# FFN weights of four chunks: split into two parts once and kept in DRAM, instead of split anew for every tile

## The chip, the cores and the metric

The kernel runs on one core of a Trainium2 chip. The core has TensorE (matrix products, with a separate stage that loads the stationary operand), VectorE (DVE), ScalarE (ACT), GpSimd (POOL) and SyncE (SP); 16 DMA engines move data between DRAM and the on-chip memory, on requests that SP, ACT or GpSimd issue in their own queues, in order. The metric is the device time of one execution in microseconds (us).

## The reference

One inference step of a two-layer encoder, for 1024 prompt rows and 32 sample rows of width 1024 that share all weights, in float32. Layer 0 mixes rows with a gated unit (SGU), layer 1 with pooling over trailing windows. Each layer then runs a channel MLP (FFN) with 4096 hidden units:

```
mod = jax.nn.silu(c) @ w_ada[i] + b_ada[i]
h = rmsnorm(x, g_norm[i, 0]) * (1 + sc1) + sh1
mix = sgu_mixer(h, ...) if i == 0 else pool_mixer(h, ...)
x = x + gt1 * rmsnorm(mix, g_norm[i, 1])
h = rmsnorm(x, g_norm[i, 2]) * (1 + sc2) + sh2
f = jnp.square(jax.nn.relu(h @ ffn_w_up[i])) @ ffn_w_down[i]
x = x + gt2 * rmsnorm(f, g_norm[i, 3])
```

The six vectors sh, sc and gt of a layer come from mod, a product with w_ada.

## The kernel before, in words

**Precision.** Each float32 operand of a large product is split into a high part, rounded to the type float32r that TensorE takes, and a low part, the rest. A product is three products: high x high, high x low, low x high (`products`, L718 to L720). A weight item is 128 x 1024 numbers, 512 KB. `do_w` (L334) splits it: ACT copies it to `wh` with rounding (L337), DVE subtracts to get `wl` (L338). `wh` and `wl` live in 16 slots of one pool (`W_SLOTS`), which is 8 items, exactly one FFN chunk.

**Tiles and chunks.** The 1056 columns are worked in three tiles of 384, 384 and 288 columns. The 4096 hidden units are worked in 8 chunks of 512; a chunk has 4 `up` items and 4 `dn` items of weights. For one chunk and one tile, `ffn_item` does 4 up steps (24 matmuls each, result `pf`; ACT squares the relu and makes the high part `fh`, DVE makes the low part `fl`) and then 8 down steps (12 matmuls each, result `pg`, which DVE adds to the sum `acc`, L870). That is 192 matmuls, called a visit here.

**Order.** `passes` lists (layer, chunk, tiles). Chunks 0 to 5 of layer 0 run over all three tiles (the steady part), so their weights are loaded and split once. Then comes a stage that runs tile by tile: chunks 6 and 7 of layer 0 for tile 0, then for tile 1, then for tile 2; then chunks 0 and 1 of layer 1 in the same way: 12 visits. Chunks 2 to 7 of layer 1 run over all tiles again. In the tile-by-tile stage a tile's last layer-0 products end early, so that its residual sum, norms, pooling and modulation can run while TensorE works on other tiles. Since the slots hold one chunk, each of the 12 visits loads and splits its 8 items again: 96 of them, where 32 are distinct.

**What is woven in.** All weights, the modulation weights (`ada` items: 16 DVE instructions per pair of items, L407 and L409) and the input rows stand in one list, `stream`, in a fixed order. `issue` puts their loads on SP's queue, as far as three raw buffers allow (`RAW_SLOTS`). After each up step and every second down step, `weave` takes one item from the stream and subtracts its assumed cost (1.1 for a weight item) from a budget (3.0 or 1.3); what is left of the budget goes to `fillers`, generators that do the residual sum, norms, pooling and modulation of a tile piece by piece (`residual`: loads `xo` from the DRAM buffer `xd`, L639 and L667; statistics through TensorE, `pn`, L620; pooling products `pp`, L1204, with weights `wg`). A weight item may only be taken when the item 8 before it has been used for the last time (`stream_ready`). `finish` runs a filler to its end where its result is needed next. The order that results is laid out when the program is built, and every engine follows its own list in order.

The 48 layer-1 `ada` items stand in the stream behind the chunks of passes 1 to 5, ten to a chunk.

Of the kernel before, what the change touches and what calls it, by code (L numbers as in the profile page):

```python
# [9 lines left out]
F32 = mybir.dt.float32  # L10
F32R = mybir.dt.float32r
AF = mybir.ActivationFunctionType
ALU = mybir.AluOpType
AX = mybir.AxisListType

P = 128
# [11 lines left out]
NT = len(TILES)  # L28
# [6 lines left out]
def tile_stream_encoder_step(  # L35
# [25 lines left out]
    nc = tc.nc  # L61
    act = nc.scalar.activation
    tt = nc.vector.tensor_tensor
# [4 lines left out]
    def pool(name, **kw):  # L68
        return ctx.enter_context(tc.tile_pool(name=name, bufs=1, reuse_waits="tile", **kw))

    const = pool("const")
    work = pool("work")
    psum = pool("psum", space=bass.MemoryType.PSUM)
    dram = pool("dram", space=bass.MemoryType.DRAM)
# [56 lines left out]
    def t_raw(name):  # L131
        return work.tile([P, 1024], F32, tag="raw", bufs=RAW_SLOTS, name=name)
# [13 lines left out]
    for i, parts in enumerate(rows):  # L146
        n = sum(k for _, k in parts)
# [36 lines left out]
    stream = []  # L184
    witem = {}

    def add_w(key, ap, shape):
        stream.append(("w", key, ap, shape))

    def add_ada(l, j):  # L190

        sl, q = j // 2, j % 2
        stream.append(
            (
                "ada",
                (l, sl, q),
                w_ada[l][q * 512 : (q + 1) * 512, sl * 256 : (sl + 1) * 256].rearrange(
                    "(k p) f -> p k f", p=P
                ),
                (4, 256),  # L200
            )
        )
# [35 lines left out]
                (2, 512),  # L238
            )

    def w_chunk(n):
        l, c, _ = passes[n]
        for j in range(4):
            f = 4 * c + j
            add_w(
                ("up", n, j),
                ffn_w_up[l][:, f * P : (f + 1) * P].rearrange("(k p) f -> p k f", p=P),
                (8, P),
            )
        for q in range(4):  # L250
            add_w(
                ("dn", n, q),
                ffn_w_down[l][c * 512 : (c + 1) * 512, q * 256 : (q + 1) * 256].rearrange(
                    "(j p) d -> p j d", p=P
                ),
                (4, 256),
            )

    every = list(range(NT))
    passes = [(0, c, every) for c in range(6)]
# [6 lines left out]
    def some_ada(n):  # L269
        for _ in range(min(n, len(rest))):  # L270
            add_ada(*rest.pop(0))
# [11 lines left out]
    first_ada = len(stream)  # L283
# [10 lines left out]
            some_ada(2)  # L294
    some_ada(99)
    rest += [(1, j) for j in (*range(8, 16), *range(8), *range(16, 48))]
    for n in range(len(passes)):
        w_chunk(n)
        if n > 0:
            some_ada(10)  # L300
    some_ada(99)

    worder = [s[1] for s in stream if s[0] == "w"]
# [2 lines left out]
    raws = {}  # L306
    loads = {}
    state = {"issued": 0, "next": 0, "raw": 0}
    deferred = []

    def in_raw(k):
        return not (stream[k][0] == "ada" and k < first_ada)

    def issue():
        while state["issued"] < len(stream):
            k = state["issued"]
            kind, key, ap, shape = stream[k]
            if in_raw(k):
                if state["raw"] == RAW_SLOTS:
                    return  # L320
                state["raw"] += 1
                r = t_raw(f"raw{k}")
            else:
                r = work.tile([P, 1024], F32, tag="W", bufs=W_SLOTS, name=f"raw{k}")
            if kind == "x":
                nr = P if key < 8 else DEC
                i = nc.sync.dma_start(r[:nr, :], ap)
            else:
                i = nc.sync.dma_start(r.rearrange("p (a b) -> p a b", a=shape[0]), ap)
            raws[k] = r  # L330
            loads[key] = i.ins
            state["issued"] += 1

    def do_w(key, r):  # L334
        wh = work.tile([P, 1024], F32R, tag="W", bufs=W_SLOTS, name="wh_" + "_".join(map(str, key)))
        wl = work.tile([P, 1024], F32R, tag="W", bufs=W_SLOTS, name="wl_" + "_".join(map(str, key)))
        act(out=wh, in_=r, func=AF.Copy)  # L337
        tt(out=wl, in0=r, in1=wh.bitcast(F32), op=ALU.subtract)  # L338
        witem[key] = (wh, wl)

    ada_acc = {}

# [97 lines left out]
    def run_deferred():  # L440
        for _ in range(len(deferred)):
            deferred.pop(0)()
# [3 lines left out]
    def do_x(b, r):  # L446
        t = min(b // 3, 2)
        c0 = (b - 3 * t) * P
        nr = P if b < 8 else DEC
        act(  # L450
            out=junk[:nr, :, :P],
            in_=r[:nr, :].rearrange("p (a b) -> p a b", b=P),
            func=AF.Square,
            accum_out=ssx[:nr, b : b + 1],
        )
        for half in range(2):
            pt = ps_ms(f"xT{b}_{half}")
            for i in range(4):
                k = half * 4 + i
                nc.tensor.transpose(  # L460
                    pt[:, i * nr : (i + 1) * nr], r[:nr, k * P : (k + 1) * P], ident[:nr, :nr]
                )
            nc.vector.tensor_copy(
                acc[t][:, half * 4 : half * 4 + 4, HALO + c0 : HALO + c0 + nr],
                pt[:, : 4 * nr].rearrange("p (a b) -> p a b", a=4),
            )
# [10 lines left out]
    def stream_step():  # L477

        k = state["next"]
        kind, key, ap, shape = stream[k]  # L480
        issue()
        run_deferred()
        r = raws.pop(k)
        if kind == "w":
            do_w(key, r)
        elif kind == "ada":
            (do_ada_pe if k < first_ada else do_ada)(*key, r)
        else:
            do_x(key, r)
        state["next"] += 1  # L490
        if in_raw(k):
            state["raw"] -= 1
        issue()
        return {"w": 1.1, "ada": 2.6, "x": 1.2}[kind]

    def need_w(key):
        while key not in witem:
            assert stream_ready(), key
            stream_step()
        return witem[key]  # L500

    def need_ada(l, which):
        k = max(i for i, s in enumerate(stream) if s[0] == "ada" and s[1] == (l, which * 4 + 3, 1))
        while state["next"] <= k:
            assert stream_ready()
            stream_step()
        run_deferred()
        run_deferred()
# [26 lines left out]
    def weave(budget, streams=1):  # L535
        if streams:
            n = 0
            run_deferred()
            while n < streams and stream_ready():
                budget -= stream_step()  # L540
                n += 1
        while budget > 0 and fillers:
            budget -= pull()
# [789 lines left out]
```

## Time and profile before

| | |
|---|---|
| median of 3 runs | 2262.3 us (2260.45 to 2263.41) |
| profiled execution | 2264.7 us, its span 2262.9 us |
| TensorE busy | 2209.5 us (98% of the span) |
| DVE busy | 1311.8 us (58%) |
| ACT busy | 869.9 us (38%) |
| GpSimd busy | 0.7 us |
| granted TensorE clock, mean | 0.989 |
| DMA | 244.16 MB, mean 108 GB/s |

Matmuls overlap in the records, so that a busy TensorE is not one at its peak: its waits and its clock have to be read too. The slices of the page cut the span into 40 parts of 56.6 us; digits are busy tenths. A row of windows gives, for a stretch of the span, the busy time of each engine with the number of instructions in brackets, then the granted clock, the busy share of the 16 DMA engines and the rate. A row of waits gives the total, the number and the longest of one kind of wait. A DMA row gives the number of transfers, the size of one and the median time from issue to landing.

### The profile page before, as it was taken

Reading aid. Unit: us, or ns where it says so; the run is one execution under the profiler, and the core shown is the slowest. Engines: PE = TensorE matmul, PEld = TensorE weight load, DVE = VectorE, ACT = ScalarE, POOL = GpSimd, SP = SyncE. Lnnn points to the kernel's source line nnn. Section 1 sums busy time; section 2 is a strip of 40 time slices with the busy share of each in tenths; the row PEclk is TensorE's granted clock in tenths of the full one; section 3 lists DMA queues with packets and bytes.
Section 4 is the critical chain, followed back from the end, with each engine's and each line's share of the span. In section 5 each row is a group of like instructions: output and inputs, shape, how many; then the busy total and the mean of one; then the engine's idle time right before and its main releaser. Section 6 shows DMA issues by size and latency. Waiting matters only on the chain.

```text
span 2262.9 us, 33417 instructions
## 1 busy us (share of the span) xinstructions
PE 2209.5 (98%) x13480; PEld 2102.8 (93%) x13480; DVE 1311.8 (58%) x2678; ACT 869.9 (38%) x1586; POOL 0.7 (0%) x6
## 2 busy tenths in 40 slices
PE   7999999999999999999999999899999999999998
PEld 4777899999989999999999999789899999999997
DVE  4855756555688366584664579999752322323345
ACT  4633431122256413223232466676552322313334
POOL 0000000000000000000000000000000000000000
PEclk9999999999999999999999999899999999999998
DMA  8465532122143223232332455564550211202112
GB/s 292 148 223 161 177 98 87 59 69 69 53 131 107 94 84 112 85 122 94 94 103 73 137 156 154 181 200 144 155 168 10 66 38 38 75 10 66 47 47 87
DMA packets 268767, 244.16 MB, mean 108 GB/s; under 512 B 8514, under 2 KB 247562, under 8 KB 268484
## 3 DMA queue, kind: packets, MB, share of 16 engines
q1 hardware_dynamic: 268340, 241.91, 34.2%
q8 instruction: 106, 1.74, 0.3%
q14 instruction: 49, 0.40, 0.1%
q10 hardware_dynamic: 272, 0.10, 0.0%
HBM read 211.32 MB, written 30.66 MB: 107 GB/s over the span
## 4 chain that ended last, share of the span: by engine, by line
PE 90%; DVE 4%; ACT 2%; DMA 2%; issue 1%; SPq 0%; DVEq 0%; ACTq 0%
PE pg L718 10%; PE pf L718 10%; PE pg L719 10%; PE pf L719 10%; PE pg L720 10%; PE pf L720 10%; PE pu L718 3%; PE po L718 3%; PE pu L719 3%; PE po L720 3%; PE po L719 3%; PE pu L720 3%; PE pv L743 2%; PE pv L744 2%; PE pv L745 2%; PE psp L924 1%
## 5 line engine op out<-in xcount | busy, mean ns | idle before, releaser
L718 PE MATMUL pf<-hh,wh_up 128*128 128x384 f32 (+1 forms) x1536 | 499.6, 326 | 4.3 <-ACT hh L693 3.7
L718 PE MATMUL pg<-fh,wh_dn 128*128 128x384 f32 (+1 forms) x1536 | 498.6, 326 | 3.6 <-DVE acc L870 3.6
L719 PE MATMUL pf<-hl,wh_up 128*128 128x384 f32 (+1 forms) x1536 | 498.3, 325 | 1.0 <-DVE hl L694 1.0
L719 PE MATMUL pg<-fl,wh_dn 128*128 128x384 f32 (+1 forms) x1536 | 496.8, 324 | 1.1 <-DVE fl L863 1.1
L720 PE MATMUL pf<-hh,wl_up 128*128 128x384 f32 (+1 forms) x1536 | 497.0, 324 | 0.0
L720 PE MATMUL pg<-fh,wl_dn 128*128 128x384 f32 (+1 forms) x1536 | 496.0, 323 | 0.0
L870 DVE TENSOR_TENSOR acc<-acc,pg 128x384 f32<-128x384 f32 (+1 forms) x336 | 173.6, 518 | 272.8 <-PE pg L720 271.8
L718 PEld LDWEIGHTS pf<-hh,wh_up 128*128 128x128 f32 x1536 | 289.2, 188 | 8.5 <-ACT hh L693 4.0
L718 PEld LDWEIGHTS pg<-fh,wh_dn 128*128 128x128 f32 x1536 | 290.0, 189 | 7.5 <-DVE acc L870 4.1
L719 PEld LDWEIGHTS pg<-fl,wh_dn 128*128 128x128 f32 x1536 | 290.3, 189 | 2.8 <-DVE fl L863 1.9
L719 PEld LDWEIGHTS pf<-hl,wh_up 128*128 128x128 f32 x1536 | 289.0, 188 | 1.7 <-DVE hl L694 1.4
L720 PEld LDWEIGHTS pg<-fh,wl_dn 128*128 128x128 f32 x1536 | 290.1, 189 | 0.0
L720 PEld LDWEIGHTS pf<-hh,wl_up 128*128 128x128 f32 x1536 | 289.1, 188 | 0.4
L409 DVE SCALAR_TENSOR_TENSOR aa<-raw,csil,aa 128x256 f32<-128x256 f32 x560 | 233.0, 478 | 3.0 <-DMA raw<-in_w_ada_dram 3.0
L1002 ACT ACTIVATE r<-pf 128x384 f32<-128x384 f32 (+1 forms) x192 | 87.6, 458 | 373.7 <-PE pf L720 359.7
L863 DVE TENSOR_TENSOR fl<-r,fh 128x384 fp32r<-128x384 f32 (+1 forms) x192 | 100.3, 523 | 181.1 <-ACT fh L862 166.6
L337 ACT ACTIVATE wh_up<-raw 128x1024 fp32r<-128x1024 f32 x96 | 101.6, 1058 | 263.2 <-PE pf L719 244.5
L338 DVE TENSOR_TENSOR wl_up<-raw,wh_up 128x1024 fp32r<-128x1024 f32 x96 | 117.5, 1224 | 122.3 <-ACT wh_up L337 122.2
L337 ACT ACTIVATE wh_dn<-raw 128x1024 fp32r<-128x1024 f32 x96 | 101.7, 1060 | 119.8 <-PE pg L719 106.9
L338 DVE TENSOR_TENSOR wl_dn<-raw,wh_dn 128x1024 fp32r<-128x1024 f32 x96 | 117.4, 1223 | 45.9 <-ACT wh_dn L337 45.8
L718 PE MATMUL po<-ush,wh_o 128*128 128x384 f32 (+1 forms) x384 | 127.4, 333 | 3.3 <-DVE acc L870 3.1
L718 PE MATMUL pu<-hh,wh_u 128*128 128x384 f32 (+1 forms) x384 | 126.8, 330 | 1.9 <-DVE s L940 1.6
(252 smaller groups left out, 2981.5 us busy)
## 6 DMA issues: line engine op xcount, KB each, us to landing
raw<-in_w_ada_dram SPq DMA_DIRECT2D x96, 512.0 KB, 3.8
raw<-in_ffn_w_up_dram SPq DMA_DIRECT2D x96, 512.0 KB, 4.1
raw<-in_ffn_w_down_dram SPq DMA_DIRECT2D x96, 512.0 KB, 3.4
raw<-in_sgu_w_in_dram SPq DMA_DIRECT2D x32, 512.0 KB, 4.6
xd<-acc SPq DMA_DIRECT2D x8, 1536.0 KB, 7.0
xo_r<-xd SPq DMA_DIRECT2D x32, 384.0 KB, 3.5
vd<-vt SPq DMA_DIRECT2D x32, 256.0 KB, 2.7
raw<-in_sgu_w_out_dram SPq DMA_DIRECT2D x16, 512.0 KB, 3.6
```

What stands on the lines that cost most here:

```text
L337: act(out=wh, in_=r, func=AF.Copy)
L338: tt(out=wl, in0=r, in1=wh.bitcast(F32), op=ALU.subtract)
L409: stt(out=aa[:, v, :], in0=w, scalar=k, in1=aa[:, v, :], op0=ALU.mult, op1=ALU.add)
L718: mm(ps[:, :n], wh, rh, start=i == 0, stop=False)
L719: mm(ps[:, :n], wh, rl, start=False, stop=False)
L720: mm(ps[:, :n], wl, rh, start=False, stop=i == last)
L743: mm(ps[:m, :], a_h, wh[:, o : o + 512], start=k == 0, stop=False)
L744: mm(ps[:m, :], a_h, wl[:, o : o + 512], start=False, stop=False)
L745: mm(ps[:m, :], a_l, wh[:, o : o + 512], start=False, stop=k == KB - 1)
L863: tt(out=dst_lo[:, :n], in0=src[:, :n], in1=dst_hi[:, :n].bitcast(F32), op=ALU.subtract)
L870: tt(out=A(t, d), in0=A(t, d), in1=ps[:, :n], op=ALU.add)
L1002: act(out=r[:, :n], in_=ps[:, :n], func=AF.Relu)
```

## The change

The four chunks of the tile-by-tile stage are split once, ahead of time. 32 new `split` items stand in the stream behind passes 1 to 5 (7, 7, 7, 7, 4). A `split` item is loaded into a raw buffer by SP as before; ACT writes its high part in three pieces of 384, 384 and 256 columns into the three buffers tagged "c"; DVE writes the low part over the raw buffer, piece by piece; GpSimd's queue stores the three high pieces and then the low part into two DRAM tiles of that item. In the tile-by-tile stage an item is no longer loaded raw and split: `do_w` has GpSimd's queue load `wh` and `wl` straight into their slots, two loads of 512 KB. Such an item takes no raw buffer and its step in the stream counts 0.1.

The layer-1 `ada` items change places: eight instead of ten behind each of passes 1 to 5, and the last eight behind the layer-1 chunks that run over all tiles, two to a chunk.

```diff
+    def some_ahead(n):
+        for _ in range(min(n, len(ahead))):
+            key, ap, shape = ahead.pop(0)
+            kept[key] = [
+                dram.tile([P, 1024], F32R, name=f"kept{i}_" + "_".join(map(str, key))) for i in range(2)
+            ]
+            stream.append(("split", key, ap, shape))
...
+    for l, c in ((0, 6), (0, 7), (1, 0), (1, 1)):
+        ahead += [((l, c, *k), ap, shape) for k, ap, shape in chunk_items(l, c)]
     for n in range(len(passes)):
         w_chunk(n)
-        if n > 0:
-            some_ada(10)
+        if 0 < n < 6:
+            some_ada(8)
+            some_ahead(7)
+        elif passes[n][0] == 1 and len(passes[n][2]) == NT:
+            some_ada(2)
     some_ada(99)
...
     def in_raw(k):
-        return not (stream[k][0] == "ada" and k < first_ada)
+        return not (stream[k][0] == "ada" and k < first_ada or stream[k][1] in kept_of)
...
     def do_w(key, r):
         wh = work.tile([P, 1024], F32R, tag="W", bufs=W_SLOTS, name="wh_" + "_".join(map(str, key)))
         wl = work.tile([P, 1024], F32R, tag="W", bufs=W_SLOTS, name="wl_" + "_".join(map(str, key)))
+        if r is None:
+            for x, src in zip((wh, wl), kept[kept_of[key]]):
+                nc.gpsimd.dma_start(x, src)
+            witem[key] = (wh, wl)
+            return
         act(out=wh, in_=r, func=AF.Copy)
         tt(out=wl, in0=r, in1=wh.bitcast(F32), op=ALU.subtract)
         witem[key] = (wh, wl)
+
+    def do_split(key, r):
+        lo = r.bitcast(F32R)
+        for c0 in range(0, 1024, 384):
+            c = slice(c0, min(c0 + 384, 1024))
+            hi = work.tile([P, 384], F32R, tag="c", bufs=3, name=f"lowh{c0}")[:, : c.stop - c0]
+            act(out=hi, in_=r[:, c], func=AF.Copy)
+            tt(out=lo[:, c], in0=r[:, c], in1=hi.bitcast(F32), op=ALU.subtract)
+            nc.gpsimd.dma_start(kept[key][0][:, c], hi)
+        nc.gpsimd.dma_start(kept[key][1], lo)
...
-        return {"w": 1.1, "ada": 2.6, "x": 1.2}[kind]
+        return 0.1 if split_before else {"w": 1.1, "split": 1.1, "ada": 2.6, "x": 1.2}[kind]
```

More of the change, by code (lines that the diff above doesn't have):

```diff
@@ L239, in w_group, with chunk_items @@
             )
-    def w_chunk(n):
-        l, c, _ = passes[n]
+    def chunk_items(l, c):
         for j in range(4):
             f = 4 * c + j
-            add_w(
-                ("up", n, j),
+            yield (
+                ("up", j),
                 ffn_w_up[l][:, f * P : (f + 1) * P].rearrange("(k p) f -> p k f", p=P),
@@ L250, in w_chunk @@
         for q in range(4):
-            add_w(
-                ("dn", n, q),
+            yield (
+                ("dn", q),
                 ffn_w_down[l][c * 512 : (c + 1) * 512, q * 256 : (q + 1) * 256].rearrange(
@@ L257, in w_chunk @@
             )
+    kept = {}
+    def w_chunk(n):
+        l, c, tiles = passes[n]
+        for (kind, j), ap, shape in chunk_items(l, c):
+            add_w((kind, n, j), ap, shape)
+            if len(tiles) < NT:
+                kept_of[(kind, n, j)] = (l, c, kind, j)
+    kept_of = {}
+    ahead = []
+    def some_ahead(n):
[5 more added lines that the diff above has]
+            stream.append(("split", key, ap, shape))
     every = list(range(NT))
@@ L317, in issue @@
             kind, key, ap, shape = stream[k]
+            if key in kept_of:
+                raws[k] = None
+                state["issued"] += 1
+                continue
             if in_raw(k):
@@ L480, in stream_step @@
         kind, key, ap, shape = stream[k]
+        split_before = key in kept_of
         issue()
@@ L485, in stream_step @@
             do_w(key, r)
+        elif kind == "split":
+            do_split(key, r)
         elif kind == "ada":
```

## The prediction

> **What bounds the kernel now.** I read the page's busy table and slices first, then a table of stages, then who TensorE waited for, then the chain.
>
> ```profile
> PE 2209.5 (98%) x13480; PEld 2102.8 (93%) x13480; DVE 1311.8 (58%) x2678; ACT 869.9 (38%) x1586; POOL 0.7 (0%) x6
> PE   7999999999999999999999999899999999999998
> DVE  4855756555688366584664579999752322323345
> ```
>
> TensorE is the bound; it dips at the start, the end and in slice 26, where DVE's digits are 9. The next table (stage; PE, weight loads, DVE, ACT, POOL busy; granted clock; DMA share; GB/s) has layer 0's steady chunks, the stage that runs tile by tile with the loads that feed it, and layer 1's steady chunks.
>
> ```profile
> 775.00:1230.00 455.00, 455.00 (x2935) 443.63 (x2934) 277.28 (x644) 122.55 (x231) 0.00 (x0) 1.00 0.32 99
> 1230.00:1690.00 460.00, 444.73 (x2649) 424.97 (x2648) 359.91 (x594) 277.16 (x479) 0.00 (x0) 0.98 0.52 160
> 1690.00:2230.00 540.00, 539.84 (x3362) 539.40 (x3361) 176.77 (x285) 156.98 (x279) 0.00 (x0) 1.00 0.15 45
> ```
>
> Only the middle stage loses TensorE time. Its worst windows (same columns), and all waits of TensorE in 1225 to 1700 us (us in total, times, longest):
>
> ```profile
> 1400.00:1425.00 25.00, 22.93 (x157) 22.51 (x156) 22.98 (x36) 15.86 (x28) 0.00 (x0) 0.94 0.71 214
> 1425.00:1450.00 25.00, 24.08 (x168) 23.04 (x167) 24.01 (x42) 13.80 (x22) 0.00 (x0) 0.99 0.48 140
> 1450.00:1475.00 25.00, 18.71 (x103) 17.10 (x103) 22.76 (x38) 16.30 (x30) 0.00 (x0) 0.80 0.47 150
> 1600.00:1625.00 25.00, 21.34 (x105) 19.25 (x104) 19.09 (x40) 13.94 (x27) 0.00 (x0) 0.90 0.40 121
> 1625.00:1650.00 25.00, 25.00 (x169) 25.00 (x168) 20.69 (x48) 16.40 (x34) 0.00 (x0) 0.96 0.51 154
> ```
>
> ```profile
> PE pf L718 <- ACT hh L693: 3.7, 1, 3.7
> PE pg L718 <- DVE acc L870: 3.6, 1, 3.6
> PE pn_r_0x L620 <- ACT sc_r_0x L605: 2.1, 1, 2.1
> PE pn_r_1x L620 <- ACT sc_r_1x L605: 1.4, 1, 1.4
> PE pp L1204 <- DMA wg<-in_pool_w_grp_dram: 1.3, 1, 1.3
> PE pg L719 <- DVE fl L863: 1.1, 2, 0.6
> PE pf L719 <- DVE hl L694: 1.0, 1, 1.0
> PE pn_rf L620 <- ACT sc_rf L605: 0.9, 1, 0.9
> ```
>
> These waits make 15.1 us, and the clock, where it was under 1.00, costs (0.06 + 0.01 + 0.20 + 0.10 + 0.04) x 25 = 10.3 us: a ceiling of 25.4 us. Nearly every wait is for DVE or ACT, late because DVE is full. The chain of waits there shows the splits among DVE's work:
>
> ```profile
> 1393.04 1.07 ACT wh_dn L337
> 1394.13 1.24 DVE wl_dn L338
> 1395.39 3.39 DMA raw<-in_ffn_w_up_dram
> 1398.78 0.54 DVE r_rp L627
> 1399.32 1.13 DVE wl_dn L338
> ```
>
> **What the tile-by-tile stage loses and gains.** 12 visits x 8 = 96 splits leave it. By stage, DVE's L338:
>
> ```profile
> 775.00:1230.00 455.00, 43.34 (x36) 1.00 0.32 99
> 1230.00:1690.00 460.00, 124.57 (x102) 0.98 0.52 160
> ```
>
> 96 x 1.22 = 117 us of DVE's 360 go (78% of the stage busy becomes about 243 / 435 = 56%), and 96 x 1.06 = 102 us of ACT. Since a step of the stream now counts 0.1 instead of 1.1, the fillers (residual, pooling, modulation) get the freed budget. In the built order, between a tile's last statistics product of layer 1's mixer and its first layer-1 FFN product, 151, 75 and 27 matmuls stood for tiles 0, 1, 2; now 281, 276 and 211. At 0.13 to 0.17 us each, tile 2's cover goes from some 4 us to 28 us. So the hh, hl, acc and fl waits and the clock dips behind them go. I keep as not recovered the three waits for sc (4.4 us: short chains of single instructions) and the one for wg (1.3 us): 25.4 - 5.7 = 19.7 us gained. What is late next if something is: those statistics chains.
>
> **The loads that take the splits' place.** Each split item becomes two GpSimd loads of 512 KB: 192 loads, 100.7 MB. The rows of stage and rate:
>
> ```profile
> q1 hardware_dynamic: 91054, 73.09, 52.1%
> raw<-in_ffn_w_down_dram SPq DMA_DIRECT2D x52, 512.0 KB, 4.2
> raw<-in_ffn_w_up_dram SPq DMA_DIRECT2D x50, 512.0 KB, 4.1
> 1257.20:1274.00 16.80, 16.80 (x98) 16.80 (x97) 7.15 (x9) 8.54 (x13) 0.00 (x0) 1.00 0.46 137
> 1650.40:1663.20 12.80, 12.80 (x99) 12.66 (x97) 6.56 (x7) 8.42 (x16) 0.00 (x0) 1.00 0.69 207
> 2204.00:2207.50 3.50, 3.50 (x23) 3.50 (x22) 0.56 (x1) 1.41 (x3) 0.00 (x0) 1.00 1.01 404
> ```
>
> The stage moved 73.1 MB, 53.5 of them raw weights (102 x 0.524); 19.6 MB of residual traffic stay. Now 120.3 MB must move in about 435 us, 277 GB/s. The old pace at full share is 73.1 / (0.521 x 460) = 305 GB/s with its pieces of 512 to 1536 B; the last row, stores in rows of 4 KB like the kept tiles', did 404. So the 16 engines suffice on average, at 69 to 91% busy. A visit has 2 x 96 matmuls: 33.6 us at 384 columns, 25.6 at 288, so 8.4 MB are wanted at 250 and 328 GB/s. Two narrow visits in a row at 305 GB/s come out 16.8 / 0.305 - 51.2 = 4 us late; the slots hold a whole visit ahead, which covers it. 435 / 192 = 2.27 us is the time one load may take from GpSimd, 4.5 us a pair.
>
> What GpSimd needs to issue one is not in this trace. From below, SP's issue of a like transfer:
>
> ```profile
> L639 SPq DMA_DIRECT2D xo_r<-xd x24: 319/339/1098, 1335.0 to 1623.9; - x24
> out_dram<-yo SPq DMA_DIRECT2D x6, 512.0 KB, 3.0
> ```
>
> 0.34 us (median of min/median/max). From above, one load after the other, 4.2 us each: 192 x 4.2 = 806 us, 371 us more than 435. I take a value under 1.2 us, since issue is the like act and lies near the lower row, the built order lets eight loads be in flight, and landing times overlap. Then nothing is added. The page "DMA: Bandwidth & Descriptors" of the Trainium skill, section "Anatomy of one DMA — SWDGE (gpsimd) path", gives 2.0 us plus bytes / 436e3 for one DMA of this queue, an estimate of 3.2 us for 512 KB: one at a time that would be 614 us for the 192 and some 180 us more than the stage has, overlapped it costs nothing; no row here shows which.
>
> Queues: SP loses the 96 raw loads; its 24 residual loads no longer stand behind raw loads that wait for DVE:
>
> ```profile
> SPq L329 <- DVE wl_dn L338: 141.8, 39, 13.2
> SPq L329 <- DVE wl_up L338: 141.5, 47, 19.4
> ```
>
> GpSimd's queue is in order: a load waits for TensorE to free its slot, and all later loads behind it, which are wanted later anyway.
>
> **The steady part pays.** 32 new splits, each in three pieces, and 8 of 48 layer-1 modulation items moved to layer 1's chunks.
>
> ```profile
> L409 DVE SCALAR_TENSOR_TENSOR aa<-raw,csil,aa 128x256 f32<-128x256 f32 x336 | 140.0, 479 | 0.0
> L407 DVE TENSOR_SCALAR aa<-raw,csil 128x256 f32<-128x256 f32 x48 | 15.1, 349 | 15.9 <-PE ada L417 15.7 <-DMA raw<-in_w_ada_dram 0.2
> L863 DVE TENSOR_TENSOR fl<-r,fh 128x384 fp32r<-128x384 f32 (+1 forms) x57 | 30.0, 526 | 30.2 <-ACT fh L862 29.4
> L862 ACT ACTIVATE fh<-r 128x384 fp32r<-128x384 f32 (+1 forms) x56 | 28.1, 501 | 1.8
> ```
>
> A split costs DVE 0.53 + 0.53 + 0.37 = 1.43 us and ACT 0.50 + 0.50 + 0.36 = 1.36 (384, 384, 256 columns): 46 and 44 us. The moved items take 8 x (7 x 0.479 + 0.349) = 29.6 us of DVE to layer 1, where it is busy 177 of 540 us. Layer 0's steady DVE goes from 277 to 293 of 455, ACT from 123 to 167: hidden behind TensorE. If that cover went, the 16 us would be the price. A raw slot is now held through load 4.1, split about 1.5 and store 3.0 = 8.6 us; three slots and a step every 24 matmuls (4.2 us) allow 12.6. A split has four stores, so GpSimd may take 1.05 us each without falling behind, and about 1.2 us with one chunk's slack (7 splits x 0.6 = 4.2 us, one step). A bound from below is a gain of nothing there (TensorE has no wait to give back); from above, at 2.27 us a store, 32 x (9.1 - 4.2) = 157 us. I take zero.
>
> **Sum.** Against the profiled execution's own time, 2264.7 us (span 2262.9 and 1.8 around it): -19.7 + 0 + 0 = 2245.0. The median of the runs is 2.4 lower, so 2243.
>
> **Rivals.** (a) The kept loads become the bound, slower. Mechanism: a load takes GpSimd or the engines longer than 2.27 us in the tile-by-tile stage, and TensorE waits for wh or wl. At half of the 404 GB/s, kept loads need 498 us and the rest 19.6 / 0.305 = 64: the stage takes 562 instead of 460, 2364 us. It breaks even where the stage takes its old 460 us, 2.4 us a load, and is only reached if issue costs seven times SP's 0.34 or the rate falls under 262 GB/s. The same skill page, section "SWDGE vs HWDGE vs iDMA", says a float32r destination always casts and only GpSimd's queue does that; it gives no rate for it, and no row of before has such a transfer. Chance 0.24.
>
> (b) The loads hold, but the steady part pays: four stores a split at 1.5 us are 6 us for a 4.2 us step; 32 x 1.8 = 58 less five chunks x 4.2 of slack = 37 us, and 2243 + 37 = 2280. For it: three buffers for the high pieces, each held through a store, 3.0 us at 512 KB, and ACT waits in order, with the relu behind it. Against: ACT is idle 73% there. Chance 0.17.
>
> (c) No change that shows: the fillers, compressed, fill DVE as before, and the gain stays under 4.5 us: 2258 to 2267. Against: 117 us less of DVE work. Chance 0.09.
>
> **Numbers.** Forecast 0.50, (a) 0.24, (b) 0.17, (c) 0.09. 0.2%, 4.5 us, is about what a measurement of this kernel can tell. Faster 0.50, same 0.09, slower 0.41. The likeliest case alone spans 2237 (all 25.4 us) to 2257; with both signs heavy, the range runs from 2235 to 2320: it holds (b) and the mild part of (a), and leaves out most of (a) from its half rate on, about 0.15, and 0.03 below.
>
> **What would show it.** Right: DVE about 240 us busy in the tile-by-tile stage, TensorE's waits there under 8 us, no clock under 0.95 there; DMA share 0.7 to 0.9; no TensorE wait in layer 0's steady chunks. Wrong by (a): TensorE waits for DMA on wh or wl, and the stage is longer than 460 us. Wrong by (b): ACT waits for stores of lowh, SP for stores of raw, and the steady windows show TensorE under 25 of 25.

## The result, and the profile after

| | before | after |
|---|---|---|
| median | 2262.7 us (2260.45 to 2263.41) | 2341.4 us (2338.68 to 2343.53) |
| ratio, 95% interval | | 1.0347 (1.0334 to 1.0360) |
| span of the profiled execution | 2262.9 us | 2337.8 us |
| DVE busy over the span | 1311.8 us | 1247.9 us |

The kernel is 79 us slower, where 19 us less were forecast. First the page of the changed kernel: busy time of the engines, two rows of slices (one digit is 58 us now), and GpSimd's DMA queue with packets, MB and the share of 16 engines.

```profile
PE 2228.7 (95%) x13480; PEld 2113.7 (90%) x13480; DVE 1247.9 (53%) x2678; ACT 819.0 (35%) x1586; POOL 172.5 (7%) x326
PE   7999999999989989999899998969999999999998
DVE  5846656555784647565573166765323424423345
q0 software_dynamic: 46080, 134.24, 17.8%
```

DVE did 64 us less; by the prediction's prices (117 of splits gone, 46 added) it would be 71. TensorE dips in slices 12, 15, 20, 25 and 27; before, only slice 26 stood out between the ends. The table of stages of the changed kernel, columns as in the prediction: layer 0's steady chunks, the tile-by-tile stage (now until 1765), layer 1's steady chunks.

```profile
775.00:1230.00 455.00, 431.27 (x2706) 415.04 (x2705) 280.39 (x635) 148.07 (x299) 61.37 (x115) 0.99 0.62 184
1230.00:1765.00 535.00, 486.11 (x2838) 464.16 (x2837) 269.63 (x532) 199.90 (x406) 110.42 (x205) 0.94 0.74 246
1765.00:2305.00 540.00, 539.85 (x3383) 537.48 (x3381) 199.15 (x356) 156.57 (x282) 0.00 (x0) 1.00 0.17 51
```

Both stages that the change touches lost: the steady part, where TensorE was busy 455.00 of 455 before, and the tile-by-tile stage, whose clock fell to 0.94 while DVE was busy only half of the time. The third stage pays nothing for its eight moved `ada` items.

A measure for the comparisons below, counted from all matmul records of a trace: the **loss** of a stage is the sum, over its matmuls, of the time from one start to the next less the pitch of that width at full clock (0.173 us for 384 columns, 0.1325 for 288). Waits and slow clock are both in it. Its zero is not exact (the steady part of the kernel before, where TensorE is always busy, comes out at -5), so that only its differences are read. The steady part is 775 to 1250 us, the tile-by-tile stage 1250 to 1775.

| loss, us | steady | tile by tile | whole span |
|---|---|---|---|
| before | -5.0 | 30.5 | 77.9 |
| after | 32.0 | 72.1 | 152.8 |

The whole difference, 74.9 us, is that of the spans (2337.8 - 2262.9). The steady part loses 37.0 more and the tile-by-tile stage 41.6; the rest of the span gives 3.7 back.

**The steady part.** Who waited for whom in 775 to 1230 us of the changed kernel (us in total, times, longest), and then the chain of waits at the first row of splits (start, us, what):

```profile
ACT lowh L380 <- DMA kept_up<-lowh: 36.3, 18, 3.3
PE pg L765 <- DVE acc L917: 19.6, 13, 3.0
ACT lowh L380 <- DMA kept_dn<-lowh: 17.1, 8, 4.2
```

```profile
818.94 3.77 DMA kept_up<-lowh
822.78 0.52 ACT lowh L380
...
823.71 4.25 DMA kept_up<-lowh
828.03 0.44 ACT lowh L380
828.47 0.46 ACT r L1049
...
836.37 7.11 DMA kept_dn<-raw
843.53 5.12 DMA raw<-in_ffn_w_up_dram
...
850.99 0.47 DVE acc L917
851.51 0.44 PE pg L765
```

A store holds a buffer of a high piece, ACT waits for it with the relu queued behind, and then a store of a low part holds the raw buffer into which the next weights should come. TensorE is reached through DVE's sums.

**The tile-by-tile stage.** TensorE's longest wait in 1230 to 1765 us, and with it DVE's waits for the residual's store; then pieces of the chain of waits in 1365 to 1660 us:

```profile
PE pg L765 <- DVE acc L917: 30.9, 5, 18.3
DVE acc L731 <- DMA xd<-acc: 23.5, 3, 11.5
DVE acc L1153 <- DMA xd<-acc: 9.2, 3, 5.4
```

```profile
1373.41 12.74 DMA xd<-acc
1386.26 4.32 DVE acc L1153 x8
...
1439.39 14.23 DMA xd<-acc
1453.72 1.68 DVE acc L731 x3
...
1529.08 19.74 DMA xd<-acc
1548.92 1.68 DVE acc L731 x3
```

`xd<-acc` stores a tile's residual sum to DRAM on SP's queue; the modulation (L731) then overwrites that sum in place, so DVE must wait for the store, and the FFN's sums (L917) wait behind it in DVE's queue. In the kernel before DVE waits for no such store, and none stood in the prediction's chain. Landing times in this stage (transfers, KB, median us), first of the changed kernel, then of the kernel before:

```profile
wh_up<-kept_up POOLq DMA_DIRECT2D x48, 512.0 KB, 4.0
wl_up<-kept_up POOLq DMA_DIRECT2D x48, 512.0 KB, 5.2
xd<-acc SPq DMA_DIRECT2D x4, 1536.0 KB, 12.7
xd<-acc SPq DMA_DIRECT2D x2, 1152.0 KB, 10.5
```

```profile
xd<-acc SPq DMA_DIRECT2D x4, 1536.0 KB, 7.3
xd<-acc SPq DMA_DIRECT2D x2, 1152.0 KB, 5.9
```

The kept loads arrive in time: TensorE waits for none. Beside them the stores land late; that the loads are the reason is tested below, by a run without them. While a store is under way the engines are full, as two windows of the changed kernel show (share 1.08 and 1.05, 385 and 363 GB/s):

```profile
1440.00:1453.00 13.00, 13.00 (x79) 12.91 (x80) 7.25 (x14) 4.75 (x10) 4.29 (x8) 1.00 1.08 385
1530.00:1548.00 18.00, 8.53 (x63) 8.20 (x62) 6.58 (x15) 3.57 (x9) 3.23 (x6) 0.86 1.05 363
```

That requests of GpSimd and SP meet on the same 16 engines is what the Trainium skill states ("DMA: Bandwidth & Descriptors", section "Issuing engines are not separate DMA queues"); these windows agree.

### The profile page after: what moved, and what is told of

The parts are those of the page before. It is cut to its first block, busy times and chain, and to the rows that moved or that the text cites. A ratio compares the mean times of both kernels' runs of the same rounds, so it can differ in the third digit from the quotient of the medians.

```text
span 2337.8 us, 33925 instructions
## 1 busy us (share of the span) xinstructions
PE 2228.7 (95%) x13480; PEld 2113.7 (90%) x13480; DVE 1247.9 (53%) x2678; ACT 819.0 (35%) x1586; POOL 172.5 (7%) x326
## 4 chain that ended last, share of the span: by engine, by line
PE 74%; DMA 9%; DVE 7%; ACT 3%; issue 2%; POOL 0%; SPq 0%; POOLq 0%; ACTq 0%; DVEq 0%
PE pf L765 9%; PE pf L766 9%; PE pf L767 9%; PE pg L765 9%; PE pg L766 9%; PE pg L767 8%; DMA xd<-acc 3%; PE pu L765 3%; PE po L765 3%; PE pu L766 3%; PE pu L767 2%; PE po L766 2%; PE po L767 2%; DMA kept_up<-lowh 1%; PE psp L971 1%
## 5 line engine op out<-in xcount | busy, mean ns | idle before, releaser
L765 PE MATMUL pg<-fh,wh_dn 128*128 128x384 f32 (+1 forms) x1536 | 506.0, 330 | 58.8 <-DVE acc L917 50.5
L917 DVE TENSOR_TENSOR acc<-acc,pg 128x384 f32<-128x384 f32 (+1 forms) x336 | 172.9, 519 | 274.2 <-PE pg L767 274.0
L766 PE MATMUL pu<-hl,wh_u 128*128 128x384 f32 (+1 forms) x384 | 124.9, 325 | 0.0
L767 PE MATMUL pu<-hh,wl_u 128*128 128x384 f32 (+1 forms) x384 | 124.7, 325 | 0.0
L766 PE MATMUL po<-usl,wh_o 128*128 128x384 f32 (+1 forms) x384 | 123.7, 322 | 0.0
L767 PE MATMUL po<-ush,wl_o 128*128 128x384 f32 (+1 forms) x384 | 123.4, 322 | 0.0
```

The lines of the kernel that those rows point to most:

```text
L765: mm(ps[:, :n], wh, rh, start=i == 0, stop=False)
L766: mm(ps[:, :n], wh, rl, start=False, stop=False)
L767: mm(ps[:, :n], wl, rh, start=False, stop=i == last)
L917: tt(out=A(t, d), in0=A(t, d), in1=ps[:, :n], op=ALU.add)
```

## The experiments

Two theories stood at the start. A: the 79 us are two prices that add, splitting and storing in the steady part, and traffic that delays the residual's stores in the other stage. B: they hang together, and one edit would bring most of it back. Times are medians; a difference is against the kernel before run beside it.

### The two parts alone

`e1_steady_alone` keeps splits and stores, and has the tile-by-tile stage load and split as before:

```diff
-            if len(tiles) < NT:
-                kept_of[(kind, n, j)] = (l, c, kind, j)
```

> The steady half alone: the 32 items are split and stored in layer 0's steady chunks as in the changed kernel, but the tile-by-tile stage loads raw weights and splits them as before; nothing reads the stored tiles. Theory A (the prices of the two stages add; the steady one is about 32 us, as the steady stage of the changed kernel lost that much to waits): 2290 to 2300 us. Rival B (the steady loss only appears together with the later loads, or is an order effect of them): 2260 to 2270 us.

2294.7 us, ratio 1.0150 (1.0128 to 1.0171): +33.6 us. Loss: steady 31.0, tile by tile 29.1.

`e2_loads_alone` splits one item only; all kept loads read its pair:

```diff
+            if not one_kept:
+                stream.append(("split", key, ap, shape))
+                one_kept.append(kept[key])
+            kept[key] = one_kept[0]
```

> The loads alone: one item is split and stored, and all 192 loads of the tile-by-tile stage read its two DRAM tiles; 31 of the 32 splits are left out, so the weights of that stage are not the right ones. Theory A: the tile-by-tile stage keeps its price, about 43 us, and the steady one goes: 2300 to 2312 us. Rival B (the loss in the tile-by-tile stage is carried over from late stores or a late steady part): 2240 to 2262 us.

2301.6 us, ratio 1.0180 (1.0160 to 1.0201): +40.5 us. Loss: steady -4.0, tile by tile 70.0. The two sum to 74 of 79 us, each at its own place: A holds. The prices can be studied one at a time.

### The steady part: which store is it

From e1, one kind of store is left out at a time: the low part's (`e5_no_low_store`) or the high pieces' (`e6_no_high_store`). What the stage computes is not touched, since it splits its own weights there.

```diff
-        nc.gpsimd.dma_start(kept[key][1], lo)
```

```diff
-            nc.gpsimd.dma_start(kept[key][0][:, c], hi)
```

> The steady half alone, without the store of the low part (a quarter of the items' stores by number, half by bytes; nothing reads the stored tiles here). A raw slot is then free when DVE has subtracted. Theory A1 (the steady price is ACT waiting for the three high-piece buffers, 58 us of waits, each held through a store that lands after 4 us): 2284 to 2297 us, near the 2295 of the steady half. Theory A2 (it is the raw slots, which SP waits 139 us for): 2264 to 2276 us.

> The steady half alone, without the three stores of the high pieces. ACT then never waits for a store. Theory A1 (high-piece buffers): 2264 to 2275 us. Theory A2 (raw slots): 2284 to 2297 us. If both bind in turn, neither this run nor the one without the low store comes under 2275 us.

Without the low stores 2288.3 us, 1.0113 (1.0093 to 1.0133): +25.9 us, 7.7 of the 33.6 gone. Without the high ones 2276.1 us, 1.0059 (1.0039 to 1.0080): +13.8, 19.8 gone, 1 us above the range for the high pieces alone. Neither run came under 2275 us, which was the sign that both kinds of buffer bind in turn. The high pieces' buffers are the larger part, and what is left moves to the raw buffers. e6's waits in the steady part:

```profile
ACT lowh L378 <- DMA raw<-in_ffn_w_up_dram: 26.7, 10, 5.6
ACT lowh L378 <- DMA raw<-in_ffn_w_down_dram: 23.5, 11, 4.1
```

`e4_interleave` keeps everything and only changes the order of the stream, one split behind each `ada` item:

```diff
-            some_ada(8)
-            some_ahead(7)
+            for i in range(8):
+                some_ada(1)
+                some_ahead(i < 7)
```

> The changed kernel, with the 7 splits of a chunk placed one after each modulation item instead of all behind them, so that a split has two steps (8 us) for its four stores. Theory A (the steady price is the buffers: three pieces and three raw slots held by stores that land after 4 to 5 us, in a 4.2 us step): ACT's waits for stores of lowh fall from 53 us to under 10 and the time to 2308 to 2322 us. Rival D (it is the added work or the added traffic, which stays): 2336 to 2345 us.

2345.9 us, 1.0378 (1.0361 to 1.0396): nothing gained, where 2308 to 2322 was expected. Its waits say where it went, from the pieces (ACT's waits for their stores fell from 59 us to 8 in 775 to 1270 us) to the raw buffers that the low stores hold (SP's waits for those stores rose from 137 to 201 us):

```profile
ACT lowh L381 <- DMA raw<-in_ffn_w_up_dram: 75.6, 12, 9.5
ACT lowh L381 <- DMA raw<-in_ffn_w_down_dram: 64.1, 15, 7.3
```

Of the two orders tried for 32 splits in five chunks, neither has room for both kinds of buffer.

### The tile-by-tile stage: the late store, the traffic, the pace

`e3_store_pieces` cuts the residual's store into four, each issued after its quarter of the sum:

```diff
+                if store:
+                    nc.sync.dma_start(xd[t][:, 2 * k2 : 2 * k2 + 2, :], a)
                 yield 0.9 if k2 % 2 else -0.9
-        if store:
-            nc.sync.dma_start(xd[t], acc[t][:, :, HALO:])
```

> The changed kernel, with the residual's store to xd cut in four, each quarter issued as soon as its sum is done, so that the modulation of a quarter waits for 384 KB only. Theory A (TensorE's loss in the tile-by-tile stage is DVE waiting for the 1.5 MB store, which shares the engines with the kept loads): the 56 us of xd stores on the chain fall to under 20, and the time to 2295 to 2312 us. Rival C (the loads take the bandwidth anyhow, and whatever transfer comes next is as late): 2330 to 2345 us.

2310.2 us, 1.0219 (1.0204 to 1.0235): +49 us, so 30 of the 79 are gone. Loss of the stage 41.7 instead of 72.1, and DVE waits for no residual store there. `e10_pieces_before` is the control, the same edit in the kernel before:

> The kernel before with the residual's store cut into four, each issued after its quarter, as in e3. Theory A (in the kernel before no store of the residual is on the path of the tile-by-tile stage; e3 repaired what the kept loads made): 2257 to 2266, no difference beyond 0.2%. Rival (the store in one piece costs the kernel before the same 31 us): 2230 to 2245, and then e3's gain says nothing on the change.

2262.2 us, 0.9996 (0.9987 to 1.0005): no difference. The late store was made by the change.

`e7_half_loads` halves the kept loads' rows, in case the engines share their time by rows rather than by bytes:

```diff
-                nc.gpsimd.dma_start(x, src)
+                for h in range(2):
+                    nc.gpsimd.dma_start(x[:, h * 512 : h * 512 + 512], src[:, h * 512 : h * 512 + 512])
```

> The changed kernel with each kept load cut in two column halves, so that GpSimd's queue moves rows of 2 KB instead of 4 KB, with twice the issues (0.54 us each). Theory R (a DMA engine takes one row from each queue in turn, so a store in rows of 1.5 KB beside loads in rows of 4 KB gets 1.5/5.5 of the rate, 1.57 MB / (0.27 x 370 GB/s) = 15.6 us; beside rows of 2 KB it gets 1.5/3.5, 9.9 us): the median landing of the xd stores falls from 12.7 us to 9 to 11 us and the time to 2322 to 2334 us. Rival (the queues share by what they ask for, and the engines are just full): landing stays at 12 us or more, 2336 to 2350 us.

2340.7 us, 1.0342 (1.0324 to 1.0360), as the changed kernel. e7's rows of the residual's store:

```profile
xd<-acc SPq DMA_DIRECT2D x4, 1536.0 KB, 10.7
xd<-acc SPq DMA_DIRECT2D x2, 1152.0 KB, 10.8
```

The larger store lands 2 us earlier, within the 9 to 11 us expected, and the smaller one does not; the time is the rival's, so that halving the rows gave nothing back.

`e8_hw_stores` is e3 with the splits' stores taken off GpSimd's queue:

```diff
-            nc.gpsimd.dma_start(kept[key][0][:, c], hi)
-        nc.gpsimd.dma_start(kept[key][1], lo)
+            nc.scalar.dma_start(kept[key][0][:, c].bitcast(F32), hi.bitcast(F32))
+        nc.sync.dma_start(kept[key][1].bitcast(F32), r)
```

> The changed kernel with the four-piece xd store of the earlier run, and with the steady part's stores moved off GpSimd's queue: the high pieces issued by ACT, the low part by SP. Theory A (what costs in the steady part is how long a store holds its buffer: 4.1 to 4.8 us to landing on GpSimd's queue, 3.0 for a like store on SP's): ACT's waits for high-piece buffers halve, 2285 to 2302 us. Rival (queue makes no difference, it is the added traffic): 2306 to 2316 us.

2299.8 us, 1.0165 (1.0149 to 1.0180): +37 us, 12 less than e3, nearly all of it in the steady part (loss 19.1 against 28.9). The time is in the range of the first theory, but not by its mechanism: ACT waits no shorter for the pieces (67 us in 775 to 1270 us, 59 in e3). What did shrink is SP's wait for the low part's stores, from 137 to 92 us, so that the raw buffers come free sooner; this was not tested by itself.

`e9_no_kept_loads` asks what is left of the stage when the traffic is gone. All kept items multiply with the first pair:

```diff
+        if r is None and one_pair:
+            witem[key] = one_pair[0]
+            return
```

> The changed kernel with 190 of its 192 kept loads left out: the first item loads its pair, and every later kept item multiplies with that same pair (so what is computed is not the reference's). The splits, stores, DVE's and ACT's work of both stages stay. It asks whether the 71 us that TensorE loses in the tile-by-tile stage are the price of the 100 MB that the kept loads move. Theory A (traffic: stores and reads of the residual on SP's queue share the 16 engines with the kept loads): the residual's stores land again in 6 to 7.5 us, its waits go, and what is left of the stage's loss is 10 to 20 us, less than the kernel before has there (28.6), since DVE is relieved; 2275 to 2295. Rival B (the loss is the stage's own chain of sums, stores and reads, however fast they are): 2315 to 2341.

2297.4 us, 1.0153 (1.0139 to 1.0167): +34 us, so 45 of the 79 were traffic: the residual's larger store lands after 5.8 us again, not 12.7, and no DVE wait for it is left. But the result is 2 us above A's range, and that is the finding: with no loads and with DVE relieved, the stage still loses 27.9 us, where the kernel before lost 30.5. The forecast's gain isn't there even when the loads are free. The chain of waits of e9 shows what DVE does where TensorE waits longest, and behind it stands that wait (total, times, longest):

```profile
1523.45 1.59 DVE acc L736 x3
1525.04 1.59 DVE hl L746 x3
1526.63 1.59 DVE acc L736 x3
1528.21 1.59 DVE hl L746 x3
1529.80 1.06 DVE acc L736 x2
1531.22 1.06 DVE hl L746 x2
```

```profile
PE pg L770 <- DVE acc L922: 10.8, 4, 6.7
```

These are 16 instructions of the modulation. The first 14 stand back to back, the FFN's sum (L922) comes behind them at 1530.78, and TensorE, which waits for that sum, stands still for 6.7 us until 1531.28. A filler is taken until the budget of the step is used up, and a kept item takes only 0.1 of it. `e12_no_loads_old_cost` is e9 with a kept item counted as before:

```diff
-        return 0.1 if split_before else {"w": 1.1, "split": 1.1, "ada": 2.6, "x": 1.2}[kind]
+        return {"w": 1.1, "split": 1.1, "ada": 2.6, "x": 1.2}[kind]
```

> e9 (one pair for all kept items, the other 190 kept loads left out, so what is computed is not the reference's) with one number changed back: a kept item counts 1.1 in the budget that paces the fillers, as a raw item does, instead of 0.1. e9 showed that without the traffic, and with DVE relieved by 90 us, the tile-by-tile stage still loses 25 us, nearly the kernel before's 29: what the forecast called recovered was not. Theory P (pace: at 0.1 the freed budget is spent at once on the fillers, whose runs of 16 DVE instructions stand in front of the sums of the FFN in DVE's queue): at 1.1 those runs thin out, TensorE's waits for the sums go, the stage loses 5 to 15 us; 2275 to 2288 against e9's 2297. Rival S (the stage's own short chains, whatever the pace): no change, 2293 to 2302; if the fillers now come too late, more.

2278.4 us, 1.0073 (1.0053 to 1.0093): +15 us, 19 less than e9. The stage's rows of windows, first e9, then e12, and e12's wait for the sums:

```profile
1230.00:1765.00 535.00, 519.84 (x3109) 500.97 (x3109) 288.73 (x581) 208.56 (x426) 9.61 (x18) 0.98 0.21 65
```

```profile
1230.00:1765.00 535.00, 531.58 (x3222) 514.93 (x3221) 287.41 (x573) 211.69 (x432) 8.01 (x15) 1.00 0.21 64
PE pg L769 <- DVE acc L921: 1.5, 1, 1.5
```

DVE has the same work, 287 against 289 us, and TensorE loses 8.0 us in place of 27.9: 11.7 of them are idle time (531.58 against 519.84 us busy), and the rest goes with the clock, 1.00 against 0.98. One number was changed, so it is the pace. `e14_pieces_old_cost` is the same number changed back in e3, with the traffic there:

> e3 (residual's store in pieces, all four chunks kept) with the same number changed back to 1.1. Theory P: the loss of the stage, 41 us in e3, falls by the 10 to 20 us that e12 finds, 2290 to 2300. Rival T (with the traffic there, the residual's reads and stores are late whatever the pace): 2305 to 2315.

2298.8 us, 1.0157 (1.0142 to 1.0173): +35 us, 14 less than e3; the loss of the stage falls from 41.7 to 31.5. With the traffic there, both theories hold in part: the pace is worth 10 us and more, and 23 us of loss stay that e12 does not have. Now DVE waits for the residual's reads, which it does in neither e12 nor the kernel before (a row of e14's waits):

```profile
DVE acc L708 <- DMA xo_r<-xd: 11.5, 5, 3.6
```

### Half of it

`e11_half_kept` is e3 with only the `up` halves kept (16 splits, 96 kept loads, the rest as in the kernel before); `e13_half_kept_old_cost` adds the old cost of 1.1.

```diff
-            if len(tiles) < NT:
+            if len(tiles) < NT and kind == "up":
...
-        ahead += [((l, c, *k), ap, shape) for k, ap, shape in chunk_items(l, c)]
+        ahead += [((l, c, *k), ap, shape) for k, ap, shape in chunk_items(l, c) if k[0] == "up"]
...
-            some_ahead(7)
+            some_ahead(4)
```

> e3 with only the up halves of the four chunks kept: 16 splits in layer 0's steady part instead of 32, 96 kept loads in the tile-by-tile stage instead of 192; the down halves are loaded raw and split as before. If both prices go by the number of items: e3's 49 us over the kernel before fall to about half, 2280 to 2292. If DVE's relief is worth something once half of the traffic is gone, the stage gains more than it loses: 2262 to 2278. Rival (the steady part pays by its first splits, whatever their number): 2295 to 2310.

> e11 (residual's store in pieces, only the up halves kept) with the same number changed back to 1.1. e11 took 2282, some 9 us of it in the steady part and 35 us of loss in the tile-by-tile stage. Theory P: the stage's loss falls to 15 to 20 us, 2262 to 2270, about the kernel before. Rival S: 2278 to 2288.

2281.7 us, 1.0083 (1.0070 to 1.0097), and 2273.0 us, 1.0039 (1.0025 to 1.0053). e11 is where prices by the number of items would put it; e13 falls between its two ranges. The pace is worth 9 us here; the stage's loss goes from 35.8 to 30.7, not to the 15 to 20 expected. Then the order: `e17_spread_only` is e13 with one split behind every two `ada` items, and `e15_spread_four` has a fourth buffer for the high pieces besides.

```diff
-            some_ada(8)
-            some_ahead(4)
+            for _ in range(4):
+                some_ada(2)
+                some_ahead(1)
```

> e15 without the fourth buffer: only the splits are spread. If the row of splits is the cause and three buffers do once they are spread: as e15 within 2 us, 2264 to 2270. If the buffers are the cause: near e13, 2270 to 2275.

> e13 (only the up halves kept, residual's store in pieces, a kept item counted 1.1) with two edits to the steady part: one split behind every two modulation items instead of four splits in a row behind eight, and four buffers of 384 columns for the high pieces instead of three (the room comes from two halves of another tile put into buffers that are free then). e13 took 2273 with 8 us of loss in the steady part, where ACT waits for the stores of the high pieces for 4 us at the second split of each row of four. If it is that wait and the row of splits that make it: the steady part's loss falls under 3 us, 2264 to 2269. Rival, as e4's raw slots: the wait moves to the loads of the modulation items and nothing is gained, 2271 to 2280.

2264.7 us, 1.0006 (0.9997 to 1.0015), and 2264.7 us, 1.0007 (0.9997 to 1.0017): the fourth buffer does nothing once the splits stand apart. The steady part of e17:

```profile
775.00:1230.00 455.00, 455.00 (x2920) 445.75 (x2919) 271.55 (x616) 139.09 (x274) 35.39 (x66) 1.00 0.49 146
```

TensorE is full again, with half of the splits and all of their four stores each. With 16 splits it was the row in which they stand, not what they do; with 32, e4's spreading gave nothing. Last, `e16_layer0_kept` is e15 with another half kept: all items of layer 0's two last chunks, none of layer 1's.

```diff
-            if len(tiles) < NT and kind == "up":
+            if len(tiles) < NT and l == 0:
```

> e15 with another half kept: both halves of layer 0's two last chunks, none of layer 1's two first ones; again 16 splits and 96 kept loads, but these come before 1500 us, ahead of most of the residual's reads. The kernel before loses 18 of its 29 us there between 1400 and 1475. If the relief counts where DVE is full and the kept traffic counts where the residual's reads stand: 2255 to 2263, at or under the kernel before. Rival: the loss moves on to the second half of the stage, where DVE splits as before, 2264 to 2274.

2254.0 us, 0.9958 (0.9946 to 0.9971): 9 us faster than the kernel before, 1 us below the expected range, and some 88 faster than the changed one. Its loss is -4.0 and 23.0. Its row of the stage:

```profile
1230.00:1765.00 535.00, 525.62 (x3155) 506.52 (x3154) 336.75 (x602) 256.03 (x474) 50.33 (x93) 0.99 0.60 192
```

## Why the prediction was wrong, point by point

**"-19.7 + 0 + 0 = 2245.0."** All three terms were wrong. Measured by parts: the steady part +34 (e1), the traffic +45 (after less e9), and for the relief of DVE nothing (e9 less before, 34.0, is e1's steady price).

**The 19.7 us gained.** What could be gained was sized about rightly: without the traffic and at the old pace, e12 loses 22 us less in the stage than the kernel before (8.0 against 30.5), near the ceiling of 25.4. The step that failed is that the fillers "get the freed budget" and so "the hh, hl, acc and fl waits" go. It counted the matmuls that cover a statistics chain (151, 75, 27, then 281, 276, 211) and not what a denser row of fillers does to the sums in the same queue. TensorE's wait for `hh` went and those for `sc` shrank from 4.4 to 0.9 us in the changed kernel, but the wait for `acc`, 3.6 us in the kernel before, became 10.8 in e9 and 30.9 with the traffic. Rival (c), "the fillers, compressed, fill DVE as before, and the gain stays under 4.5 us", had a chance of 0.09. Taken for the stage alone and without the traffic, its small gain is what happened (e9), but the reason is runs of fillers and not a full DVE: in 1230 to 1765 us DVE was busy 289 us in e9, and just as long in e12, which gains.

**"Then nothing is added" by the kept loads.** The parts that the prediction priced came out: GpSimd's issue, taken as under 1.2 us, is 0.54 us (a row of the changed kernel's line 368, min/median/max in ns),

```profile
L368 POOL DMA_DIRECT2D wh_up<-kept_up x48: 537/537/545, 1247.4 to 1720.4; - x48
```

and the share of the engines is 0.74, within the 0.69 to 0.91 forecast, though over a longer stage. Rival (a), late kept loads, fell: no TensorE wait for them. What failed is the sentence "So the 16 engines suffice on average": it asked whether the kept loads arrive, and kept the old landing times for everything else. The residual's store, 7.3 us before, took 12.7, and an operation that the prediction never listed, the overwriting of the sum in place, waits for it. The paragraph on queues freed SP's 24 residual loads of the raw loads ahead of them; 16 of them landed later all the same, after 5.0 us in place of 4.1, and the other 8 after 4.7 as before.

**"I take zero" for the steady part.** The mechanism of rival (b), "three buffers for the high pieces, each held through a store ... ACT waits in order, with the relu behind it", is what the waits show, and its price, 37 us, is near e1's 33.6. That is luck: the price came from stores that cost GpSimd 1.5 us each, and they cost 0.53. The term that was mis-sized is the store: 3.0 us was taken from another store; these landed after 4.0 to 4.3 us, and the low part's after 4.8 (two rows of the changed kernel, 775 to 1230 us).

```profile
kept_up<-lowh POOLq DMA_DIRECT2D x32, 192.0 KB, 4.2
kept_up<-raw POOLq DMA_DIRECT2D x16, 512.0 KB, 4.8
```

As an estimate from these rows, one round of a piece's buffer is 0.52 (ACT) + 0.53 (issue) + 4.2 = 5.2 us against a step of 4.2 us; with 3.0 it would have been 4.1 and just hidden. 32 splits times 1.0 us are 32 us; e5 and e6 show that the raw buffers have a share in the price, so that the sum fits better than it explains. Half of the splits, a row of four at a time, cost 12.5 us (e13, loss 7.5 against -5.0), and spread out 1 us (e17). The raw buffers' 8.6 us of 12.6 had the same fault: with 5.2 for the slowest kind of load, 1.5 for the split and 4.8 for the store it is 11.5, and with a store of 7.1 us, as at 836 in the chain, 13.8. The chance of 0.17 rested on "ACT is idle 73% there", an average over a part in which the splits stand in rows of seven.

**What would show it.** Of the tests the prediction named, DVE's busy time (255 us in 1261 to 1763 us, the same stretch of the program as the 460 us before; forecast 240) and the DMA share came out; TensorE's waits under 8 us and a clock not under 0.95 didn't (0.94 for the stage), and (b)'s three signs were all there.

## What to carry to other kernels

Where new transfers are to run beside old ones, price the landing of the old ones anew, and look for every instruction that waits for them, also those that only want to overwrite what is being stored. Work that is moved into a part with room is paid by how it stands there: compare the round of its buffers with the step at which it comes, not the mean load. When an engine is relieved in a woven schedule, keep the pace of what is woven in, or the freed time is spent in runs that stand in front of the work on the path.

## What was not expected of the hardware

A store on one queue lands later beside loads of another queue, even where those loads themselves come in time: 1.5 MB in 12.7 us instead of 7.3, at a mean share of 0.74. Halving the rows of the loads did not give the time back (10.7 and 10.8 us in e7 for the two sizes against 12.7 and 10.5), and a quarter of the store still took 9.4 us in e3, where a whole one took 5.8 in e9, without the loads.

```profile
xd<-acc SPq DMA_DIRECT2D x16, 384.0 KB, 9.4
```

Stores of 128 and 192 KB in the steady part of the changed kernel took 4.0 to 4.3 us to land, about as long as the loads of 512 KB there (3.4 to 5.2). And the kept loads, whose destination is float32r, showed no half rate: in the tile-by-tile stage their queue moved 104.36 MB in 58.9% of the engines' time,

```profile
q0 software_dynamic: 29541, 104.36, 58.9%
```

which is 331 GB/s at full share (104.36 / (0.589 x 535)), more than the 305 that the prediction took from the kernel before. Why e16's choice of half gains where e15's does not was expected from where the residual's reads stand, and it fits: up to 1435 us TensorE is full in both (205 of 205 us from 1230 on), and from 1435 to 1670 us, where e16 has no kept loads, it is busy 225.7 us against e15's 221.3. That place was not varied by itself.
